# Delta rule: the diagonal blocks of two heads inverted in one pass on 64 partitions

## The chip, the cores and the metric

The kernel runs on one core of a Trainium2 chip. The metric is the time of one execution on the device in microseconds. A core has a matrix engine (PE, with its weight loads shown as PEld), three engines for elementwise work (DVE is VectorE, ACT is ScalarE, POOL is GpSimd) and a queue for transfers that SyncE (SP) issues. Each engine executes its own instruction list in order and waits at semaphores for the others.

## The reference, cut to what matters

One layer of a streaming encoder, for 1024 tokens of width 1024: three mixers (chunked attention A, a Conformer convolution B, a gated delta rule C), merged by three sigmoid gates, then an output projection, a layer norm, an MLP and a second layer norm. The change is in mixer C, which has four heads of width 128:

```
    lmat = jnp.where(strict, jnp.einsum("bnihd,bnjhd->bnhij", kbeta, k) * decay, 0.0)
    tmat = lax.linalg.triangular_solve(eye + lmat, jnp.broadcast_to(eye, lmat.shape),
                                       left_side=True, lower=True, unit_diagonal=True)
    u = jnp.einsum("bnhij,bnjhd->nbhid", tmat, v * beta[..., None])
    w = jnp.einsum("bnhij,bnjhd->nbhid", tmat, kbeta * jnp.exp(gc)[..., None])
...
    def step(state, inp):
        v_new = u_c - jnp.einsum("bhcd,bhde->bhce", w_c, state)
        o_c = (jnp.einsum("bhcd,bhde->bhce", q_c * jnp.exp(g_c)[..., None], state)
               + jnp.einsum("bhij,bhje->bhie", a_c, v_new))
        state = state * jnp.exp(g_last)[..., None, None] + jnp.einsum("bhcd,bhce->bhde", k_dec, v_new)
...
    mix = sum_b sigmoid(gate_b) * (y_b @ W_branch[b])
```

The last line is from the docstring of the layer. `tmat` is the inverse of a lower triangular matrix for each chunk; `step` is a recurrence over the chunks of a head.

## The kernel before, in words

All values are f32. A large product is made of three matmuls on pieces of the operands (high by high, low by high, high by low); the low piece is a subtraction at line 116 (`xl`, `yl` and the like), mostly on DVE or POOL.

Mixer C works with 8 chunks of 128 tokens for each of its heads 0 to 3. A head goes through these steps:

- **dn_a**: `dn_proj` projects, convolves and normalises q, k, v; `dn_s1` makes the triangular matrix `LT`, the masked products `aT`, decays and scales. A row of the decays goes through DRAM and comes back spread over the partitions (L501 and L503 make it, L504 stores it, L452 loads it). The 32x32 blocks on the diagonal of `LT`, four for each of the 8 chunks, are stored to DRAM (`blk_d`, L524).
- **dn_inv**: the 32 blocks are loaded as `X`, one block per partition (L542), and inverted by substitution on DVE: 31 times a product into `tm` (L553) and a subtraction from `X` (L554), the shapes changing each time. POOL clears the upper half (L555), and the result is stored (`inv_d`, L557).
- **dn_b**: `z_load` loads the output gate. `dn_s2` loads the inverted blocks into `T`, transposes them on DVE (L587) and builds the inverse of the whole 128x128 matrix by products `px`, `py`, `px2`, `py2` on PE (all L578), whose results DVE copies out (L592 to L606), then `pu`, `pw`. `dn_scan` is the recurrence: a chunk's step is a matmul with the state (L631), a DVE subtraction (L632), a matmul for the new state (L635), a DVE update of the state `S` (L640); the output matmuls (L633, L642) and their copies on ACT (L643, L644) hang beside it. `dn_out` normalises the head's output (L648, POOL at L190, L655), transposes it on PE (`to`, L659), multiplies by the gate (L660) and stores it to DRAM (`yc_d`, L661).

The merge products follow: `merge(0)`, `merge(1)`, `merge(2)` for mixers A, B and C. Their operands are loaded back from DRAM (`yr`, L719, split into `yh` on ACT at L720 and `yl` at L116); the matmuls write `pbr` (L164 on PE; their weights are named `wbr0x` for A, `wbr1x` for B and `wbr2x` for C, with x for a block of the 1024 output channels, and four k steps are summed, one for each 128 of the 512 channels, so that k step h of C is head h); DVE multiplies by the sigmoid of the gate (L773) and adds (L775, L776). `merge(2)` thus needs the stored output of all four heads.

Two further pieces of work have no tie to the delta rule. Projections of the merge gates (`side_proj`, matmuls that write `fj`, L164 too) are issued at a low priority and put where the scheduler sees room, and so are the convolution steps of mixer B (L676 to L701). The order on each engine is fixed when the program is built: a scheduler takes the operations in program order, by priority and readiness in its own model, so a change of program order moves filling work as well.

Buffers: `dn` is a pool of the phase with one or more buffers for each name; `slot` hands out one of 30 tiles of 128x1024, shared with other stages. PSUM banks: two for `fj`, two for `pbr`, four (`m`) for the delta rule.

Of the kernel before, what the change touches and what calls it, by code (L numbers as in the profile page):

```python
# [9 lines left out]
F32 = mybir.dt.float32  # L10
# [5 lines left out]
P = 128  # L16
T = 1024
# [6 lines left out]
CH = 4  # L24
# [15 lines left out]
def bc_last(ap, n):  # L40
    return bass.AP(tensor=ap.tensor, offset=ap.offset, ap=[list(a) for a in ap.ap] + [[0, n]])


def bc_mid(ap, n):
    a = [list(x) for x in ap.ap]
    return bass.AP(tensor=ap.tensor, offset=ap.offset, ap=[a[0], [0, n]] + a[1:])
# [8 lines left out]
def hybrid_block(ctx, tc, x, xT, pT, w_in, relb, conv_w, conv_b, cln_g, cln_b, dnw, a_log, dt_bias,  # L55
# [3 lines left out]
    V, S, G, PE, SY = nc.vector, nc.scalar, nc.gpsimd, nc.tensor, nc.sync  # L59
# [6 lines left out]
    def phase(name, waits="pool"):  # L66

        if scoped[0] is not None:
            scoped[0].close()
        st = ExitStack()  # L70
        pool = st.enter_context(tc.tile_pool(name=name, bufs=1, reuse_waits=waits))
        scoped[0] = st

        def alloc(shape, dt, tag, bufs, name):
            return pool.tile(shape, dt, tag=tag, bufs=bufs, name=name)

        return alloc
# [8 lines left out]
    def slot(shape, dt=F32, name="g"):  # L86
        return gp.tile(shape, dt, tag="g", bufs=NSLOT, name=name)
# [7 lines left out]
    def bank(tag, shape=(P, 512), name="b"):  # L95
        return ps.tile(list(shape), F32, tag=tag, bufs=NBANK[tag], name=name)
# [324 lines left out]
    def dn_proj(h):  # L421
        res = []
        for i, off in enumerate((O_QC, O_KC, O_VC)):
            w = wrows(w_in, off + P * h, f"wc{h}{i}")
            cw = dnw_s[:, 4 * i + h, :]
            acc = slot([P, T], name=f"c{i}{h}")
            halo = mp.tile([P, 4], F32, tag="halo", bufs=4, name="halo")
            for hf, sl, pp in mm_b(xs, w, name="pc"):
                S.activation(acc[:, sl], pp, AF.Copy, scale=cw[:, 3:4])
                for s_ in (1, 2, 3):  # L430
                    V.scalar_tensor_tensor(acc[:, 512 * hf + s_:512 * hf + 512], pp[:, :512 - s_],  # L431
                                           cw[:, 3 - s_:4 - s_], acc[:, 512 * hf + s_:512 * hf + 512],
                                           ALU.mult, ALU.add)
                    if hf == 1:
                        V.scalar_tensor_tensor(acc[:, 512:512 + s_], halo[:, 3 - s_:3], cw[:, 3 - s_:4 - s_],
                                               acc[:, 512:512 + s_], ALU.mult, ALU.add)
                if hf == 0:
                    V.tensor_copy(halo[:, 0:3], pp[:, 509:512])
            S.activation(acc, acc, AF.Silu)
            res.append(acc)  # L440
        return res

    def ch3(t):
        return t.rearrange("p (c i) -> p c i", i=P)

    def dn_s1(h, qkv):
# [3 lines left out]
        def bcast(src, hf):  # L450
            t = dn([P, 512], F32, "sd", 4, "bc")
            SY.dma_start(t, rows_bcast(src[4 * hf:4 * hf + 1, :], 512))  # L452
            return t

        blk_d = dr.tile([NT, 4, 32, 32], F32, name=f"blk{h}")
        inv_d = dr.tile([NT, 4, 32, 32], F32, name=f"inv{h}")
        brk_d = dr.tile([NT, P], F32, name=f"brk{h}")
        nv = mp.tile([P, 6, NT], F32, tag="nv", bufs=2, name="nv")
        rq, rk, brk, begk, edk = [nv[:, i, :] for i in range(5)]
        LT = dn([P, T], F32, "LT", 1, f"LT{h}")  # L460
        aT = slot([P, T], name=f"aT{h}")
        kdec = slot([P, T], name=f"kdec{h}")
        DTs = []
        for hf in range(2):
# [11 lines left out]
            for i, src in ((1, kT), (0, qT)):  # L476
                tp = bank("pj", name="tk")
                for c4 in range(4):
                    c = hf * 4 + c4
# [3 lines left out]
                for c4 in range(4):  # L483
                    c = hf * 4 + c4
# [3 lines left out]
            for c4 in range(4):  # L488
                c = hf * 4 + c4
# [15 lines left out]
        for hf in range(2):  # L505
# [7 lines left out]
            for c4 in range(4):  # L513
                cs = slice((hf * 4 + c4) * P, (hf * 4 + c4 + 1) * P)
                PE.matmul(kk[:, c4 * P:(c4 + 1) * P], lhsT=kT[:, cs], rhs=kT[:, cs], start=True, stop=True)
            V.tensor_tensor(LT[:, sl], kk, DT, ALU.mult)
            V.tensor_tensor(LT[:, sl], LT[:, sl], bcast(brk_d, hf), ALU.mult)
            kq = bank("pj", name="kq")
# [4 lines left out]
        for d in range(4):  # L523
            SY.dma_start(blk_d[:, d].rearrange("c j i -> j c i"), ch3(LT)[32 * d:32 * d + 32, :, 32 * d:32 * d + 32])  # L524
        for hf in range(2):
# [7 lines left out]
            V.tensor_tensor(ch3(kdec)[:, c8, :], ch3(kdec)[:, c8, :], bc_last(edk[:, c8], P), ALU.mult)  # L533
        return dict(qg=qT, W=kT, vb=vT, LT=LT, aT=aT, kdec=kdec, rq=rq, blk_d=blk_d, inv_d=inv_d)

    def dn_inv(h, o):

        blk_d, inv_d = o["blk_d"], o["inv_d"]
        NB = 32

        X = dn([P, T], F32, "X", 1, "X")
        SY.dma_start(X[:NB, :], blk_d.rearrange("c d j i -> (c d) (j i)"))  # L542
        tm = dn([P, 256], F32, "tm", 1, "tm")
        Xa = X[:NB, :]
        diag = bass.AP(tensor=Xa.tensor, offset=Xa.offset, ap=[list(Xa.ap[0]), [33, 32]])
        V.memset(diag, 1.0)
        X3 = X[:NB, :].rearrange("p (r c) -> p r c", c=32)
        for jj in range(31):
            nr, ncol = 31 - jj, jj + 1
            L = X[:NB, jj * 32 + jj + 1:jj * 32 + 32]  # L550
            R = X3[:, jj, 0:ncol]
            tv = tm[:NB, :nr * ncol].rearrange("p (r c) -> p r c", c=ncol)
            V.tensor_tensor(tv, bc_last(L, ncol), bc_mid(R, nr), ALU.mult)  # L553
            V.tensor_tensor(X3[:, jj + 1:32, 0:ncol], X3[:, jj + 1:32, 0:ncol], tv, ALU.subtract)  # L554
        G.affine_select(out=X3, in_=X3, pattern=[[1, 32], [-1, 32]], compare_op=ALU.is_ge, fill=0.0, base=0,  # L555
                        channel_multiplier=0)
        SY.dma_start(inv_d.rearrange("c d i j -> (c d) (i j)"), X[:NB, :])  # L557

    def dn_s2(h, o):

        LT, inv_d = o["LT"], o["inv_d"]
        T3 = dn([P, T], F32, "T3", 1, "T3")
# [8 lines left out]
        def prod(name, lhsT, rhs, w=P):  # L571

            res = []
            for hf in hfs:
                p = bank("m", name=name)
                for c4 in range(4):
                    l, r = lhsT(hf * 4 + c4), rhs(hf * 4 + c4)
                    PE.matmul(p[0:l.shape[-1], c4 * w:(c4 + 1) * w], lhsT=l, rhs=r, start=True, stop=True)  # L578
                res.append(p.rearrange("p (c d) -> p c d", d=w)[:, 0:4, :])
            return res  # L580

        def chunk(t, c, rows=slice(0, P), c0=0, c1=P):
            return t[rows, c * P + c0:c * P + c1]
# [4 lines left out]

        px = prod("px", lambda c: chunk(LT, c), lambda c: chunk(T3, c))
        for hf in hfs:  # L590
# [24 lines left out]
    def z_load(h, o):  # L615
        z = o["z"] = slot([P, T], name=f"z{h}")
        SY.dma_start(z, z_d[h])
        S.activation(z, z, AF.Silu)
# [28 lines left out]
    def dn_out(h, o, O, ss):  # L647
        V.tensor_scalar(ss, ss, 1.0 / P, RMS_EPS, ALU.mult, ALU.add)  # L648
        r = mp.tile([P, 8], F32, tag="ss", bufs=4, name="r")
        pow_mh(r, ss, 8)  # L650
        for hf in range(2):
            sl = slice(512 * hf, 512 * hf + 512)
            c8 = slice(4 * hf, 4 * hf + 4)
            z = o["z"][:, sl]
            V.tensor_tensor(ch3(O)[:, c8, :], ch3(O)[:, c8, :], bc_last(r[:, c8], P), ALU.mult)  # L655
            tp = bank("m", name="to")
            for c4 in range(4):
                c = hf * 4 + c4
                PE.transpose(tp[:, c4 * P:(c4 + 1) * P], O[:, c * P:(c + 1) * P], ident)  # L659
            V.scalar_tensor_tensor(O[:, sl], tp, ng_s[:, 0:1], z, ALU.mult, ALU.mult)  # L660
            SY.dma_start(yc_d[h][:, sl], O[:, sl])  # L661
# [164 lines left out]
    dn = phase("dn")  # L826

    def dn_a(h):
        return dn_s1(h, dn_proj(h))

    def dn_b(h, o):
        z_load(h, o)
        dn_s2(h, o)
        dn_out(h, o, *dn_scan(h, o))

    st = [None] * CH
    st[0] = dn_a(0)
    dn_inv(0, st[0])
    for h in range(1, CH):
        st[h] = dn_a(h)  # L840
        dn_b(h - 1, st[h - 1])
        dn_inv(h, st[h])
    dn_b(CH - 1, st[CH - 1])
    merge(0, ya_d, True, False)
    merge(1, yb_d, False, False)
    merge(2, yc_d, False, True)
# [331 lines left out]
    dn = phase("down", "tile")  # L1178
# [163 lines left out]
```

## Time and profile before

| quantity | value |
|---|---|
| time, median of 3 runs | 1949.96 us (1948.24 to 1951.97) |
| time of the profiled execution | 1944.56 us |
| span of the profiled execution | 1942.8 us |
| mean granted TensorE clock, share of full | 0.982 |
| PE busy | 1850.1 us, 95% of the span |
| DVE busy | 1258.3 us, 65% |
| ACT busy | 831.1 us, 43% |
| POOL busy | 445.0 us, 23% |

The span lies within the execution's own time, which has 1.8 us around it. Shares are means over all stages; the delta rule runs from about 518 us to 1030 us after the span's start, with the first merges inside its last part.

### The profile page before, as it was taken

What the parts mean: (1) busy time and instruction counts of PE and PEld (TensorE: products, weight loads), DVE (VectorE), ACT (ScalarE), POOL (GpSimd) and SP (SyncE); (2) the same over time, 40 slices, a digit from 0 to 9 for tenths busy, and PEclk for the clock granted to TensorE, in tenths of its full rate; (3) what the DMA queues carried; (4) which work ended last, traced back from release to release, by engine and by line L of the source; (5) the groups of instructions that cost most, each with busy time, mean ns of one, the idle gap of its engine ahead of it and who ended that gap; (6) DMA issues with size and microseconds to landing.
All of it is one profiled execution on the core that took longest, in us unless ns stands there. A gap on an engine that the chain in (4) does not pass through costs nothing. (4 is left out here: it accounts for less than half of the span.)

```text
span 1942.8 us, 25812 instructions
## 1 busy us (share of the span) xinstructions
PE 1850.1 (95%) x9265; PEld 1543.4 (79%) x9265; DVE 1258.3 (65%) x2203; ACT 831.1 (43%) x1516; POOL 445.0 (23%) x373
## 2 busy tenths in 40 slices
PE   8999999989999989989999999989999989999996
PEld 7988887778777878777877997768888877878775
DVE  3248969989957857664377367763333327865978
ACT  4454544446324343442344237435555553333333
POOL 2123423334322122212121142223232310000001
PEclk9999999999999989999999999999999999999998
DMA  6212222232242332333354435763333367542442
GB/s 200 82 53 68 74 64 72 65 87 87 87 117 60 98 90 84 92 111 107 125 190 163 155 123 188 246 211 130 104 114 108 109 233 251 214 162 97 175 152 87
DMA packets 207793, 244.68 MB, mean 126 GB/s; under 512 B 23792, under 2 KB 126256, under 8 KB 207664
## 3 DMA queue, kind: packets, MB, share of 16 engines
q1 hardware_dynamic: 207664, 243.03, 38.6%
q8 instruction: 73, 1.20, 0.2%
q14 instruction: 56, 0.46, 0.1%
HBM read 183.17 MB, written 59.80 MB: 125 GB/s over the span
## 5 line engine op out<-in xcount | busy, mean ns | idle before, releaser
L676 DVE SCALAR_TENSOR_TENSOR ca<-ci,cw_s,ca 128x512 f32<-128x512 f32 x240 | 214.2, 892 | 3.8
L986 PE MATMUL pda<-bh,ah 128*128 128x512 f32 x256 | 97.6, 396 | 9.1 <-DVE x L1246 5.1
L987 PE MATMUL pda<-bl,ah 128*128 128x512 f32 x256 | 100.6, 393 | 0.0
L988 PE MATMUL pda<-bh,al 128*128 128x512 f32 x256 | 100.4, 393 | 0.0
L190 POOL TENSOR_TENSOR mv<-mv,nhalf 128x1 f32<-128x1 f32 x16 | 17.4, 1094 | 360.9 <-DVE mv L683 360.9
L307 POOL TENSOR_SCALAR st<-st,mx 128x640 f32<-128x640 f32 (+2 forms) x64 | 58.7, 919 | 179.8 <-DVE mx L306 174.2
L304 ACT ACTIVATE st<-st,mx 128x640 f32<-128x640 f32 (+2 forms) x64 | 44.5, 696 | 117.0 <-DVE mx L300 116.8
L986 PE MATMUL pdb<-bh,ah 128*128 128x512 f32 x192 | 74.6, 401 | 7.0 <-DVE x L1246 7.0
L1204 ACT ACTIVATE ah<-draw 128x1024 fp32r<-128x1024 f32 x32 | 33.9, 1061 | 102.9 <-PE pda L987 51.2
L1157 DVE TENSOR_TENSOR r<-puc,r 128x512 f32<-128x512 f32 x16 | 11.1, 692 | 103.1 <-PE puc L988 103.1
L987 PE MATMUL pdb<-bl,ah 128*128 128x512 f32 x192 | 76.4, 398 | 0.0
L988 PE MATMUL pdb<-bh,al 128*128 128x512 f32 x192 | 75.9, 398 | 0.0
L986 PEld LDWEIGHTS pda<-bh,ah 128*128 128x128 f32 x256 | 48.6, 190 | 20.9 <-ACT bh L1204 7.3
L988 PEld LDWEIGHTS pda<-bh,al 128*128 128x128 f32 x256 | 48.7, 190 | 10.4
L987 PEld LDWEIGHTS pda<-bl,ah 128*128 128x128 f32 x256 | 48.7, 190 | 10.2 <-DVE bl L116 0.2
L553 DVE TENSOR_TENSOR tm<-X 32x31 f32<-32x31 f32 (+15 forms) x124 | 53.4, 431 | 3.0
L116 DVE TENSOR_TENSOR al<-draw,ah 128x1024 fp32r<-128x1024 f32 x32 | 39.1, 1221 | 22.7 <-ACT ah L1204 22.7
L431 DVE SCALAR_TENSOR_TENSOR c<-pc,dnw_s,c 128x511 f32<-128x511 f32 (+2 forms) x72 | 52.5, 731 | 0.1
L554 DVE TENSOR_TENSOR X<-X,tm 32x31 f32<-32x31 f32 (+15 forms) x124 | 50.1, 404 | 3.0
L771 ACT ACTIVATE sgl<-sgl 128x512 f32<-128x512 f32 x48 | 30.2, 631 | 50.0 <-DMA sgl<-sg_d 41.5
L334 ACT ACTIVATE ph<-tp 128x512 fp32r<-128x512 f32 (+2 forms) x72 | 37.0, 525 | 32.0 <-PE tp L330 27.5
L116 POOL TENSOR_TENSOR wu2l<-wu,wu2h 128x512 fp32r<-128x512 f32 x16 | 20.8, 1303 | 128.1 <-ACT wu2h L866 128.1
(1605 smaller groups left out, 6199.7 us busy)
## 6 DMA issues: line engine op xcount, KB each, us to landing
draw<-h_d SPq DMA_DIRECT2D x48, 512.0 KB, 5.0
wu<-in_w_up_dram SPq DMA_DIRECT2D x32, 512.0 KB, 3.9
h_d<-r SPq DMA_DIRECT2D x64, 256.0 KB, 2.1
draw<-in_w_down_dram SPq DMA_DIRECT2D x32, 512.0 KB, 4.6
sg_d<-fs SPq DMA_DIRECT2D x48, 256.0 KB, 2.1
sgl<-sg_d SPq DMA_DIRECT2D x48, 256.0 KB, 2.8
wg<-in_w_pg_dram SPq DMA_DIRECT2D x36, 256.0 KB, 4.3
cb<-in_w_down_dram SPq DMA_DIRECT2D x16, 512.0 KB, 8.1
```

What stands on the lines that cost most here:

```text
L116: eng.tensor_tensor(lo, src, hi.bitcast(F32), ALU.subtract)
L304: S.activation(st[:, :nk], st[:, :nk], AF.Exp, scale=-1.0, bias=mx[:, nm:nm + 1], accum_out=mx[:, 2:3])
L307: G.tensor_scalar(st[:, :nk], st[:, :nk], mx[:, 3:4], 1.0, ALU.mult, ALU.mult)
L334: S.activation(ph[:, :n], tp[:, :n], AF.Copy)
L431: V.scalar_tensor_tensor(acc[:, 512 * hf + s_:512 * hf + 512], pp[:, :512 - s_], cw[:, 3 - s_:4 - s_], acc[:, 512 * hf + s_:512 * hf + 512 ...
L553: V.tensor_tensor(tv, bc_last(L, ncol), bc_mid(R, nr), ALU.mult)
L554: V.tensor_tensor(X3[:, jj + 1:32, 0:ncol], X3[:, jj + 1:32, 0:ncol], tv, ALU.subtract)
L676: V.scalar_tensor_tensor(acc, t[:, H - s_:H - s_ + 512], cw_s[:, i, H - s_:KB - s_], acc, ALU.mult, ALU.add)
L986: PE.matmul(out_, lhsT=ah, rhs=bh, start=first, stop=False, skip_group_check=True)
L987: PE.matmul(out_, lhsT=ah, rhs=bl, start=False, stop=False, skip_group_check=True)
L988: PE.matmul(out_, lhsT=al, rhs=bh, start=False, stop=last, skip_group_check=True)
L1204: S.activation(hi, src, AF.Copy)
```

## The change

`dn_inv` takes a list of two heads. Two loads fill 64 partitions of `X`, the 62 DVE operations, the memset and the mask run once for both heads, and two stores write the result. `LT` lives from `dn_a` of its head to `dn_b`, and two heads now wait between the two, so it moves from a one-buffer tile to a slot. The program order of the heads becomes a0, a1, inversion of 0 and 1, b0, a2, b1, a3, inversion of 2 and 3, b2, b3, where it was a0, inv0, a1, b0, inv1, a2, b1, inv2, a3, b2, inv3, b3.

```diff
@@ -457,7 +457,7 @@
         brk_d = dr.tile([NT, P], F32, name=f"brk{h}")
         nv = mp.tile([P, 6, NT], F32, tag="nv", bufs=2, name="nv")
         rq, rk, brk, begk, edk = [nv[:, i, :] for i in range(5)]
-        LT = dn([P, T], F32, "LT", 1, f"LT{h}")
+        LT = slot([P, T], name=f"LT{h}")
         aT = slot([P, T], name=f"aT{h}")
         kdec = slot([P, T], name=f"kdec{h}")
         DTs = []
@@ -533,13 +533,13 @@
             V.tensor_tensor(ch3(kdec)[:, c8, :], ch3(kdec)[:, c8, :], bc_last(edk[:, c8], P), ALU.mult)
         return dict(qg=qT, W=kT, vb=vT, LT=LT, aT=aT, kdec=kdec, rq=rq, blk_d=blk_d, inv_d=inv_d)
 
-    def dn_inv(h, o):
-
-        blk_d, inv_d = o["blk_d"], o["inv_d"]
-        NB = 32
+    def dn_inv(os_):
+
+        NB = 32 * len(os_)
 
         X = dn([P, T], F32, "X", 1, "X")
-        SY.dma_start(X[:NB, :], blk_d.rearrange("c d j i -> (c d) (j i)"))
+        for n, o in enumerate(os_):
+            SY.dma_start(X[32 * n:32 * n + 32, :], o["blk_d"].rearrange("c d j i -> (c d) (j i)"))
         tm = dn([P, 256], F32, "tm", 1, "tm")
         Xa = X[:NB, :]
         diag = bass.AP(tensor=Xa.tensor, offset=Xa.offset, ap=[list(Xa.ap[0]), [33, 32]])
@@ -554,7 +554,8 @@
             V.tensor_tensor(X3[:, jj + 1:32, 0:ncol], X3[:, jj + 1:32, 0:ncol], tv, ALU.subtract)
         G.affine_select(out=X3, in_=X3, pattern=[[1, 32], [-1, 32]], compare_op=ALU.is_ge, fill=0.0, base=0,
                         channel_multiplier=0)
-        SY.dma_start(inv_d.rearrange("c d i j -> (c d) (i j)"), X[:NB, :])
+        for n, o in enumerate(os_):
+            SY.dma_start(o["inv_d"].rearrange("c d i j -> (c d) (i j)"), X[32 * n:32 * n + 32, :])
 
     def dn_s2(h, o):
 
@@ -834,13 +835,15 @@
         dn_out(h, o, *dn_scan(h, o))
 
     st = [None] * CH
-    st[0] = dn_a(0)
-    dn_inv(0, st[0])
-    for h in range(1, CH):
-        st[h] = dn_a(h)
-        dn_b(h - 1, st[h - 1])
-        dn_inv(h, st[h])
-    dn_b(CH - 1, st[CH - 1])
+    st[0], st[1] = dn_a(0), dn_a(1)
+    dn_inv(st[0:2])
+    dn_b(0, st[0])
+    st[2] = dn_a(2)
+    dn_b(1, st[1])
+    st[3] = dn_a(3)
+    dn_inv(st[2:4])
+    dn_b(2, st[2])
+    dn_b(3, st[3])
     merge(0, ya_d, True, False)
     merge(1, yb_d, False, False)
     merge(2, yc_d, False, True)
```

The lines behind `dn_inv` stand one further down in the changed kernel (L631 becomes L632, L659 becomes L660, L773 becomes L774).

The list of PE during the recurrence of head 3, before (`c_7845` and `c_7768` are the k and q tiles of head 3; the matmuls before and after these rows are `pbr` too):

```order
L164 MATMUL pbr<-yh,wbr13h 128x512
L164 MATMUL pbr<-yl,wbr13h 128x512
L164 MATMUL pbr<-yh,wbr13l 128x512
L631 MATMUL scan<-S,c_7845 128x128
L633 MATMUL scano<-S,c_7768 128x128
L164 MATMUL pbr<-yh,wbr14h 128x512
L164 MATMUL pbr<-yl,wbr14h 128x512
L164 MATMUL pbr<-yh,wbr14l 128x512
```

And after, for the same recurrence, its last steps (`c_7788`, `c_7711`, `c_7634` are the v, k and q tiles of head 3), up to its output:

```order
L636 MATMUL scan<-c_7788,kdec_7859 128x128
L643 MATMUL scano<-c_7788,aT_7858 128x128
L632 MATMUL scan<-S,c_7711 128x128
L634 MATMUL scano<-S,c_7634 128x128
L636 MATMUL scan<-c_7788,kdec_7859 128x128
L643 MATMUL scano<-c_7788,aT_7858 128x128
L632 MATMUL scan<-S,c_7711 128x128
L634 MATMUL scano<-S,c_7634 128x128
L643 MATMUL scano<-c_7788,aT_7858 128x128
L660 MATMUL to<-ident,c_7788 128x128 x8
L164 MATMUL pbr<-yh,wbr20h 128x512
L164 MATMUL pbr<-yh,wbr21h 128x512
```

Between the steps there stood matmuls of the merges of A and B, and now stands nothing; the matmuls behind the output transposes `to` are those of `merge(2)`.

PE at the end of head 2, before (`c_7291` is its v tile; `T_8390`, `LT_7991` belong to head 3):

```order
L659 MATMUL to<-ident,c_7291 128x128 x8
L578 MATMUL px<-T_8390,LT_7991 128x128 x8
L164 MATMUL pbr<-yl,wbr00h 128x512
L164 MATMUL pbr<-yh,wbr00l 128x512
L164 MATMUL pbr<-yh,wbr00h 128x512
L164 MATMUL pbr<-yl,wbr00h 128x512
L164 MATMUL pbr<-yh,wbr00l 128x512
```

And after (`c_7225` is head 2's v tile, `T_8258`, `TT_8264`, `LT_7857` belong to head 3):

```order
L634 MATMUL scano<-S,c_7071 128x128
L643 MATMUL scano<-c_7225,aT_7295 128x128
L660 MATMUL to<-ident,c_7225 128x128 x8
L579 MATMUL px<-T_8258,LT_7857 128x128 x8
L579 MATMUL py<-TT_8264,T_8258 128x128 x8
L164 MATMUL pbr<-yh,wbr20h 128x512
L164 MATMUL pbr<-yh,wbr21h 128x512
L164 MATMUL pbr<-yl,wbr20h 128x512
L164 MATMUL pbr<-yh,wbr20l 128x512
```

Behind the first products of head 3 stood `merge(0)` with its weights `wbr00`, and before `py` 17 such matmuls; now `py` follows `px` directly, and then come matmuls of `merge(2)` (`wbr20`, `wbr21`), which take head 2's output as it comes back from DRAM.

DVE in the middle of an inversion, before (that of head 3; `c_7291` is head 2's v tile in its recurrence, `bst`, `bmv` belong to mixer B):

```order
L553 TENSOR_TENSOR tm<-X 32x135
L696 BN_STATS bst<-tb 128x6
L632 TENSOR_TENSOR c_7291<-c_7291,scan 128x128
L554 TENSOR_TENSOR X<-X,tm 32x27x5
L682 BN_AGGR bmv<-bst 128x2
L553 TENSOR_TENSOR tm<-X 32x156
L683 TENSOR_SCALAR bmv<-bmv 128x1
L640 SCALAR_TENSOR_TENSOR S<-S,egl,scan 128x128
```

And after, in the second of the two inversions (`mix` is the merged output, `pbr` a product of `merge(0)`):

```order
L553 TENSOR_TENSOR tm<-X 64x192
L774 TENSOR_TENSOR mix_8489<-pbr,sgl 128x512
L554 TENSOR_TENSOR X<-X,tm 64x24x8
L774 TENSOR_TENSOR mix_8530<-pbr,sgl 128x512
L774 TENSOR_TENSOR mix_8489<-pbr,sgl 128x512
L553 TENSOR_TENSOR tm<-X 64x207
L554 TENSOR_TENSOR X<-X,tm 64x23x9
L553 TENSOR_TENSOR tm<-X 64x220
```

The inversion shared DVE with the recurrence of the head before; it now shares it with the merge of A, and no recurrence runs beside it.

## Rows read from the trace of the kernel before

**Rows 1.** The page, part 1: busy time, share of the span, instructions.

```profile
PE 1850.1 (95%) x9265; PEld 1543.4 (79%) x9265; DVE 1258.3 (65%) x2203; ACT 831.1 (43%) x1516; POOL 445.0 (23%) x373
```

**Rows 2.** Two stretches: length, busy PE, PEld, DVE, ACT, POOL; clock, DMA share, GB/s.

```profile
560.00:882.00 322.00, 293.77 (x1550) 244.25 (x1550) 234.41 (x578) 124.54 (x314) 74.68 (x62) 0.95 0.31 90
882.00:1000.00 118.00, 116.75 (x593) 97.00 (x592) 49.70 (x101) 44.63 (x94) 21.35 (x16) 1.00 0.44 143
```

**Rows 3.** Waits of PE, 560 to 882: total us, times, longest us.

```profile
PE scan L631 <- DVE S L640: 7.2, 5, 3.9
PE scan L635 <- DVE c L632: 5.5, 5, 3.6
PE tv L490 <- ACT tk L485: 3.1, 1, 3.1
PE pc L164 <- DVE halo L438: 3.0, 1, 3.0
```

**Rows 4.** The page, part 5: the inversion, busy us, mean ns, idle before.

```profile
L553 DVE TENSOR_TENSOR tm<-X 32x31 f32<-32x31 f32 (+15 forms) x124 | 53.4, 431 | 3.0
...
L554 DVE TENSOR_TENSOR X<-X,tm 32x31 f32<-32x31 f32 (+15 forms) x124 | 50.1, 404 | 3.0
```

**Rows 5.** Timeline, DVE: start, duration, operation; one on 32 partitions.

```profile
925.60 0.28 DVE L597 TENSOR_SCALAR TT<-py 32x128 f32<-32x128 f32 x1 [4.23 <-PE py L578]
```

**Rows 6.** Timeline: a step of the recurrence that nothing covers.

```profile
803.66 0.35 DVE L640 SCALAR_TENSOR_TENSOR S<-S,egl,scan 128x128 f32<-128x128 f32 x1
...
804.59 0.29 DVE L632 TENSOR_TENSOR c<-c,scan 128x128 f32<-128x128 f32 x1 [0.30 <-PE scan L631]
...
804.93 0.49 PE L635 MATMUL scan<-c,kdec 128*128 128x128 f32 x2 [0.16 <-DVE c L632]
...
805.68 0.34 DVE L640 SCALAR_TENSOR_TENSOR S<-S,egl,scan 128x128 f32<-128x128 f32 x1
```

**Rows 7.** Timeline, PE: two matmuls back to back.

```profile
1028.15 0.39 PE L164 MATMUL pbr<-yh,wbr20h 128*128 128x512 f32 x1
...
1028.38 0.39 PE L164 MATMUL pbr<-yl,wbr20h 128*128 128x512 f32 x1
```

**Rows 8.** Timeline: the output of head 2.

```profile
909.53 0.39 PE L642 MATMUL scano<-c,aT 128*128 128x128 f32 x2
...
912.63 1.29 DVE L655 TENSOR_TENSOR c<-c,r 128x512 f32<-128x512 f32 x2 [1.76 <-POOL r L190]
...
917.91 1.03 PE L659 MATMUL to<-ident,c 128*128 128x128 f32 x8
```

**Rows 9.** Head 3's output through DRAM to PE; then landing times of `yc_d`.

```profile
1020.07 0.93 SPq L661 DMA_DIRECT2D yc_d<-c  x2
...
1028.84 0.50 PE L164 MATMUL pbr<-yh,wbr20h 128*128 128x512 f32 x1
...
DMA to landing us min/median/max: 2.0/4.2/6.1
```

**Rows 10.** Timeline, heads 2 and 3: decay row, start and end of an inversion, transposes.

```profile
736.43 0.28 DVE L503 COPY vr<-vp 8x128 f32<-8x128 f32 x1 [2.30 <-PE vp L501]
...
753.39 0.09 DVE L546 MEMSET X<- 32x32 f32 x1
...
833.38 0.28 DVE L503 COPY vr<-vp 8x128 f32<-8x128 f32 x1
...
853.19 0.09 DVE L546 MEMSET X<- 32x32 f32 x1
...
888.07 1.26 POOL L555 TENSOR_SCALAR_AFFINE_SELECT X<-X 32x1024 f32<-32x1024 f32 x1 [9.62 <-DVE X L554]
...
894.82 1.30 DVE L587 STREAM_TRANSPOSE TT<-T 128x512 f32<-128x512 f32 x2
```

**Rows 11.** DVE by line: the merge's product.

```profile
L773 DVE TENSOR_TENSOR mix<-pbr,sgl 128x512 f32<-128x512 f32 x16 | 10.9, 690 | 18.8 <-PE pbr L164 15.9 <-DMA sgl<-sg_d 2.3 <-ACT sgl L771 0.6
```

**Rows 12.** Timeline, PE: one matmul at the lower clock.

```profile
703.09 0.63 PE L164 MATMUL fj<-xl,fg17h 128*128 128x512 f32 x1
```

## The prediction

> **What bounds the kernel now.** The page comes first: PE is busy for 95% of the span [rows 1], so what the change does to the time is what it does to PE's idle time and to its clock. The windows come next, over the delta rule: from 560 to 882 us PE is busy for 293.77 of 322 us, so 28.2 us are idle, and its granted clock is 0.95 of full; from 882 to 1000 us it is busy for 116.75 of 118 at a clock of 1.00 [rows 2]. The second stretch holds the last part of head 2's recurrence, and head 3's products and most of its recurrence: they cost nothing there, because the merges of A and B fill every gap. The waits of PE say what the 28.2 us are: 12.7 for the steps of the recurrences (7.2 and 5.5), 3.1 for the decays of a head, 3.0 for the convolution, and small ones [rows 3]. DVE is late in them, and the inversion is part of what keeps it: 53.4 and 50.1 us in all, with 248 operations [rows 4]. So there is something to gain, but a bounded thing: 28.2 us of idle PE and, with a clock of 0.95 over 322 us, some 16 us of PE's speed.
>
> **What is removed.** Four inversions of 62 operations become two. An operation on 32 partitions with 128 elements took 0.28 us [rows 5], one on 128 partitions with 128 elements 0.29 us [rows 6]: the partitions cost nothing, so an inversion of 64 partitions takes (53.4+50.1)/4 = 25.9 us, as one of 32 did. DVE loses 51.8 us of work. The two memsets and masks that go, and the transfers, whose number stays (a load and a store for each head), are off PE's path; `LT` in a slot costs nothing where no slot has to be waited for, and the order shows no operation that is put off for one. I price these at 0; a late slot would cost what a late head costs, below.
>
> **What is moved, and its price.** PE's list keeps its work: the same matmuls, 1850 us. What moves is the filling. Before, nine to twenty matmuls of the merges of A and B stand in each half step of head 3's recurrence. Now the merge of A stands under the second inversion and the merge of B under head 2, and nothing is left for head 3: its 30 matmuls stand back to back, behind them `to`, and behind that `merge(2)`, which needs `to`'s result. I sum this tail as path less PE's own work.
>
> A step that nothing covers took from one state update to the next 2.02 us, with other DVE work in it; its four parts alone are 0.49, 0.29, 0.49 and 0.35 (L631's matmul taken like L635's), so 1.62 [rows 6]. I take 1.85, since a semaphore stands between the parts. PE's own work in a step is two pairs of 0.39 [rows 8].
> - Head 2's last 2.5 steps, for which the filling has run out: 4.6 less 2.0 is 2.7.
> - Head 2's output: from the last product to the scaling 3.1 us (909.53 to 912.63), half of the scaling 0.65, the transposes 1.03 [rows 8] and hops of 0.2: 5.0, less 1.0, is 4.0. Before, this had cover.
> - Head 3's products. On PE, `px` and `py` go ahead, and then 12 matmuls of `merge(2)` that take head 2's output through DRAM; `px2` stands behind the first of them, and on DVE two of head 3's small transposes stand behind the two splits of that output. From the store to the first matmul head 3's trip took 8.8 us (1020.07 to 1028.84); two transfers at the shortest landing, 2.0 each, and about 1 for the split between make 5 [rows 9]. I take 7. The rest, with 0.7 for the second split [rows 11], is the exchange of PE and DVE from `py` to `pw`: I estimate 7.4, from halves of groups of 1.03 [rows 8] and copies near 0.3 [rows 5] with hops. Together 15.1, less PE's six groups of 1.03 and 12 matmuls at 0.23 [rows 7], 9.0, is 6.1.
> - Head 3's recurrence: 0.9 for the first chunk and six more steps, 12.0, less 15 pairs of 0.39, 5.9, is 6.1.
> - Its output and trip: 5.0 and 7.0, less 1.0, is 11.0. PE can't run ahead of it, for `merge(2)` has two `pbr` banks, both of which stand waiting for the last k step, head 3.
>
> The tail is 30 us (24 with steps of 1.62 and trips of 5; 35 with 2.02 and 8.8).
>
> Then the two inversions, each of which now keeps two heads waiting. From the decay row to the inversion it took 19.8 us for head 3 and 17.0 for head 2, mean 18.4; from its mask to the first transposes 6.8 (888.07 to 894.82) [rows 10].
> - Second one: 18.4 + 25.9 + 6.8, and about 19 of the merge's and split's operations on DVE between them at 0.69 [rows 11], 13.1: 64 us from head 3's decay row to head 2's `px`. In this piece PE has 192 matmuls of the merge of A at 0.23 [rows 7], 44.2, and 4.2 of small ones: 48. Idle: 16.
> - First one: 18.4 + 25.9 + 6.8 and 8 of convolution work on DVE, 59, against 192 matmuls at 0.23 and 30 small ones, 48. Idle: 11.
> - What stays as it was: 3.1 for a head's decays and 3.0 for the convolution [rows 3], about 6.5 for the recurrences of heads 0 and 1 (half of 12.7, since DVE has no inversion beside them), 1.5 for head 2's products.
>
> That is 41 us against 28.2 before, so 13 more. Clock: a matmul at the lower level took 0.63 us [rows 12] where the same form takes 0.39 [rows 7]; I count 4 us of PE work after the tail at that rate, 2.5 more. Sum: 30 + 13 + 2.5 = 45. The profiled execution took 1944.56 us, so 1990; the median of the runs is 5.4 us above that execution, which I leave in the range.
>
> **The Trainium skill against the trace.** The Trainium skill, "VectorE: DVE Perf Modes", section "Rules for kernel authors", says that for a chain of VectorE operations the number of operations is what to bring down. The trace agrees as far as [rows 5, 6] go. By it the change should gain; that is the faster rival below. The Trainium skill, "TensorE: Matmul & The Clock Gate", section "What's actually happening", says that the matrix engine is throttled by default and that activity lifts this, which speaks against a tail full of gaps. The trace agrees: 0.95 in the stretch with 28.2 us idle and 1.00 in the full one [rows 2]. By it the tail runs at 1.2 GHz; that is the dear rival.
>
> **The rivals.**
> - *The tail alone.* The new waits at the inversions are repaid by the 51.8 us that DVE loses: heads 0 and 1 run with a freer DVE, and PE's idle there stays at 28 or falls to 15. For it: DVE is busy for 234 of 322 us in that stretch, and its lateness is 12.7 us of waits [rows 2, 3]. Against it: the 18.4 before an inversion and the 6.8 after are transfers and queues, which do not shrink. Time: 1944.6 + 24 to 35, less up to 13: 1960 to 1976.
> - *The dear tail.* The clock falls in the tail. Then a matmul takes 1.6 times as long (0.63 for 0.39) [rows 7, 12], 0.8 for 0.49 [rows 6]: the 17 on the path of the two recurrences add 0.3 each, 5; the eight groups of 1.03 on the path add 0.6 each, 5; the matmuls of `merge(2)` add 3. That is 13 more: 2003, to 2016 with the tail's upper bound and 8 more at the inversions. For it: the gaps there come one behind the other. Against it: in the recurrences before, with waits of up to 3.9 us [rows 3], the clock over the whole stretch stayed at 0.95.
> - *Faster.* The shorter DVE list ends the waits of the recurrences and of the decays and lifts the clock: at most 28.2 + 16 us are there. The place is 560 to 882; it decides from the point at which it saves more than the tail's 24 to 35, and PE must then be idle there for less than about 3 us. Against it: the waits for the two inversions are in that very stretch. If all of it were saved and the tail were at its lower end, 1944.6 + 24 - 44 = 1925; in the middle about 1935.
> - *Nothing.* The tail is covered by work that the order does not show as such, or the savings equal it: 1945 to 1955.
>
> **How the numbers follow.** Chances: the forecast, 1976 to 2003, 0.58; the tail alone 0.15; the dear tail 0.18; faster 0.05; nothing 0.04. The likeliest is 1990. The range leaves out the two last, 0.09, and the outer quarter of the two beside the forecast, 0.08: 1964 to 2014. A measurement of this kernel tells about 0.2%, 4 us, from no change: faster 0.05, within it 0.04, slower 0.91.
>
> **What would show it.** In the profile after: DVE's busy time near 1258 - 52 = 1206 us; 62 + 62 operations of the inversion with a mean near 420 ns; PE's busy share near 93%; waits of PE for head 3's state and for `yh` near the end of the delta rule, with a sum near 25 to 35 us where the stretch of [rows 2] had 1.2; two waits of PE's `px` for the transposes or for the inverted blocks, 16 and 11 us long. It is wrong if PE's order as built does not lead to waits, that is if the stretch of head 3 has steps well under 1.6 us, or if the wait for the second inversion is near 0.

## The result, and the profile after

The changed kernel takes 1977.45 us (median of 4 runs, 1975.45 to 1980.25) against 1949.85 before: 1.0142 times, 95% interval 1.0124 to 1.016, so 27.6 us slower. The forecast was 1990, in a range of 1964 to 2014. The profiled execution has a span of 1973.7 us, 30.9 more than before. Two disturbed runs, one of 3083 us of a later experiment and one of 6460 us of the kernel before, count in no time and no ratio below.

The first view is the page of the changed kernel: busy time, share of the span, instructions; then the two groups of the inversion.

```profile
PE 1859.3 (94%) x9265; PEld 1552.0 (79%) x9265; DVE 1204.1 (61%) x2077; ACT 833.5 (42%) x1515; POOL 445.4 (23%) x371
...
L554 DVE TENSOR_TENSOR X<-X,tm 64x31 f32<-64x31 f32 (+15 forms) x62 | 25.8, 416 | 1.5
L553 DVE TENSOR_TENSOR tm<-X 64x31 f32<-64x31 f32 (+15 forms) x62 | 24.5, 395 | 1.7
```

The change does on DVE what it says: half the operations at the same 0.4 us each, on twice the partitions; DVE is busy for 54.2 us less than in [rows 1]. And it is slower all the same. PE has the same 9265 records; it is idle for 1973.7 - 1859.3 = 114.4 us, against 1942.8 - 1850.1 = 92.7 before, 21.7 more; and its busy time is 9.2 longer, from stretches at a lower clock and from matmuls that stand alone. The two make the 30.9.

The windows of the changed kernel say where. Columns as in [rows 2]; the cuts are head 1's decay row (620.4), head 0's products (686), head 0's and head 1's outputs (768, 872), head 3's decay row (882), head 2's products (948), and a time near the end of its recurrence (1010).

```profile
518.00:620.40 102.40, 99.28 (x468) 80.84 (x467) 47.68 (x102) 38.35 (x89) 29.47 (x25) 0.98 0.32 92
620.40:686.00 65.60, 53.57 (x244) 43.50 (x244) 47.30 (x115) 17.87 (x31) 14.42 (x13) 0.92 0.40 107
686.00:768.00 82.00, 79.35 (x439) 66.43 (x439) 27.91 (x69) 29.60 (x81) 18.05 (x16) 1.00 0.28 82
768.00:872.00 104.00, 104.00 (x564) 87.21 (x563) 42.54 (x109) 40.44 (x104) 23.51 (x20) 1.00 0.29 89
872.00:882.00 10.00, 2.63 (x18) 1.99 (x16) 3.02 (x10) 7.09 (x22) 2.91 (x1) 0.80 0.33 108
882.00:948.00 66.00, 53.99 (x233) 44.38 (x233) 48.54 (x111) 24.00 (x37) 12.23 (x9) 0.89 0.55 167
948.00:1010.00 62.00, 61.38 (x323) 51.19 (x323) 40.37 (x68) 24.01 (x48) 11.39 (x9) 0.99 0.48 150
1010.00:1068.00 58.00, 41.25 (x232) 33.32 (x231) 23.79 (x55) 14.70 (x46) 3.61 (x3) 0.83 0.14 46
```

Three stretches stand out. Under each of the two inversions PE is idle for 12.0 us (65.60 - 53.57, 66.00 - 53.99), and for 7.4 just before the second. In the last row, the end of head 2 and head 3's own stretch, it is idle for 16.8 us of 58, at a clock of 0.83. Between them PE is nearly full (2.65 us idle from 686 to 872, 0.62 from 948 to 1010). DVE is never near full: 48.54 of 66 us at most.

The waits of PE from 518 to 1060 us, columns as in [rows 3]; the smaller of the two waits for `yh` is the start of a longer one, cut off at 1060:

```profile
PE pbr L164 <- ACT yh L721: 10.2, 2, 9.5
PE tq L702 <- DVE bcv L699: 8.6, 2, 8.4
PE to L660 <- DVE c L656: 6.9, 2, 3.5
PE tv L490 <- ACT tk L485: 4.7, 1, 4.7
PE kk L515 <- DVE c L492: 3.0, 1, 3.0
PE vp L501 <- DVE nv L497: 2.7, 1, 2.7
PE scan L632 <- DVE S L641: 2.5, 10, 0.6
PE px L579 <- DMA T<-inv: 2.4, 1, 2.4
```

The recurrence waits of [rows 3], 12.7 us, are down to some 5, in many short pieces: with no inversion beside them the steps are answered at once. In their place stand waits for other things that are late: the operand of the merge of A, the norm of mixer B, each head's output. The timeline of the tail shows the pieces of it in order:

```profile
1024.47 3.62 PE L579 MATMUL px<-T,LT 128*128 128x128 f32 x16
...
1027.88 2.12 PE L579 MATMUL py<-TT,T 128*128 128x128 f32 x16
...
1038.71 1.95 PE L579 MATMUL pw<-TT,c 128*128 128x128 f32 x16
...
1041.64 0.49 PE L632 MATMUL scan<-S,c 128*128 128x128 f32 x2 [0.54 <-DVE S L639]
...
1043.51 0.49 PE L632 MATMUL scan<-S,c 128*128 128x128 f32 x2 [0.22 <-DVE S L641]
...
1057.38 1.97 PE L660 MATMUL to<-ident,c 128*128 128x128 f32 x8 [3.45 <-DVE c L656]
1065.08 0.80 PE L164 MATMUL pbr<-yh,wbr20h 128*128 128x512 f32 x1 [5.74 <-ACT yh L721]
```

A bare step takes about 1.8 us (43.51 - 41.64 is 1.87, the next five 1.81 on average); head 3's output waits 3.45 us for its scaling, is transposed in 1.97 where [rows 8] had 1.03, and comes back from DRAM 5.74 us later. The first matmul of the last k step takes 0.80 us where [rows 7] has 0.39: PE is at the lower of its levels, 1.2 GHz, after these gaps: its granted clock is 0.50 from 1065.08 to 1069 us.

### The profile page after: what moved, and what is told of

Read it like the earlier page. It is cut to its first block, busy times and chain, and to the rows that moved or that the text cites. A ratio compares the mean times of both kernels' runs of the same rounds, so it can differ in the third digit from the quotient of the medians.

```text
span 1973.7 us, 25685 instructions
## 1 busy us (share of the span) xinstructions
PE 1859.3 (94%) x9265; PEld 1552.0 (79%) x9265; DVE 1204.1 (61%) x2077; ACT 833.5 (42%) x1515; POOL 445.4 (23%) x371
## 5 line engine op out<-in xcount | busy, mean ns | idle before, releaser
L990 PEld LDWEIGHTS pda<-bl,ah 128*128 128x128 f32 x256 | 48.7, 190 | 10.2
L989 PEld LDWEIGHTS pdb<-bh,ah 128*128 128x128 f32 x192 | 37.2, 194 | 16.0 <-issue 8.2
L116 DVE TENSOR_TENSOR pl<-tp,ph 128x512 fp32r<-128x512 f32 (+2 forms) x72 | 42.4, 593 | 8.8 <-ACT ph L334 8.1
```

What stands on the lines that cost most here:

```text
L116: eng.tensor_tensor(lo, src, hi.bitcast(F32), ALU.subtract)
L989: PE.matmul(out_, lhsT=ah, rhs=bh, start=first, stop=False, skip_group_check=True)
L990: PE.matmul(out_, lhsT=ah, rhs=bl, start=False, stop=False, skip_group_check=True)
```

## The experiments

The theory that they set out from: the joint inversion makes head 2 wait until head 3 has its decays and its blocks. The delta rule's way through the heads, which was half hidden, becomes one chain from head 3's decays to its output; PE's filling is spent under the wait, and the end of the chain stands bare. The rivals: the new order of the heads or the slots cost; or the length of the shared inversion does. All times are medians; ratios are to the kernel before, with 95% intervals.

**Order and slots without the grouping.**

```diff
-    dn_inv(st[0:2])
+    dn_inv(st[0:1])
+    dn_inv(st[1:2])
...
-    dn_inv(st[2:4])
+    dn_inv(st[2:3])
+    dn_inv(st[3:4])
```

> The program order of the heads and LT in a slot stay as in the changed kernel, but each head has an inversion of its own on 32 partitions. My theory (the joint inversion makes head 2 wait for head 3, and the filling work is used up under that wait, so that head 3's products, recurrence and output stand bare): the list of PE has matmuls of the merges in head 3's recurrence again, and the time is that of the kernel before, 1945 to 1958 us. Rival (the new order of the heads, or two LT in slots, costs): it stays near the changed kernel, 1970 to 1980 us.

Measured: 1949.54 us, ratio 1.0002 (0.9988 to 1.0017). The program order of the heads and two more slots cost nothing: the scheduler goes by what is ready, and puts each head's inversion under the head before it, as in the kernel before (the four inversions begin at 568.9, 655.4, 759.7 and 858.8 us; before at 569.5, 652.1, 753.4 and 853.2). The whole price is that one instruction works for two heads.

**The inversion made shorter, and longer.** In the second inversion alone, 1 step of 31, or the 31 steps twice:

```diff
-    def dn_inv(os_):
+    def dn_inv(os_, steps=31):
...
-        for jj in range(31):
+        for jj in range(steps):
...
-    dn_inv(st[2:4])
+    dn_inv(st[2:4], 1)
```

> The second inversion does 1 of its 31 steps (the output of heads 2 and 3 is not the reference's); the rest as in the changed kernel. It takes 25 us of DVE work off the way from head 3's decays to head 2's first product. My theory (the price lies in the bare tail of head 3, which this leaves as it is, and in the wait for the operand of the merge of A at the start of that stretch): little is won, 1966 to 1977 us. Rival (the two heads' wait for a long inversion is the price): the time falls by the 25 us, to about 1952.

```diff
-    def dn_inv(os_):
+    def dn_inv(os_, rep=1):
...
-        for jj in range(31):
+        for jj in list(range(31)) * rep:
...
-    dn_inv(st[2:4])
+    dn_inv(st[2:4], 2)
```

> The second inversion's 31 steps are done twice in a row (the output of heads 2 and 3 is not the reference's), 26 us more of DVE work between head 3's decays and head 2's first product. My theory (from head 3's decays to the end nothing else but this chain sets the time): nearly all of it is seen, 1996 to 2006 us, since the filling is used up anyhow. Rival (PE's filling covers the inversion, and its length hardly counts): below 1988 us.

Measured: 1964.96 us (1.0078, 1.0049 to 1.0107) and 2000.41 (1.0254, 1.0233 to 1.0276). The longer one is as expected, 23 of its 26 us are seen. In its timeline PE has spent the merge of A and a part of that of B, and then stands:

```profile
980.35 2.90 PE L579 MATMUL px<-T,LT 128*128 128x128 f32 x12 [17.92 <-DMA T<-inv]
```

The shorter one gives back 12.5 us of its 25, one more than the most I expected and half of what the rival said: I had not counted that with `px` earlier (911.7 in place of 946.4 us) 48 of the 192 matmuls of the merge of A are spent ahead of it in place of all of them, and more are left for head 2 (its trace has no wait before head 2's output). The wait of 9.4 us at the start and the bare tail of head 3 stay. So the inversion's length counts nearly fully upward and by half downward: at its present length it is on the chain. What stops the gain at half was not taken apart.

**Heads 2 and 3 through the recurrence in turn.**

```diff
-    dn_b(2, st[2])
-    dn_b(3, st[3])
+    dn_bb([(2, st[2]), (3, st[3])])
...
+    def dn_bb(hos):
+        for h, o in hos:
+            z_load(h, o)
+            dn_s2(h, o)
+        dn_scans(hos)
+        for h, o in hos:
+            dn_out(h, o, o["vb"], o["ss"])
```

`dn_scans` is `dn_scan` with the loop over heads inside that over chunks, and two `S` tiles for each head.

> Heads 2 and 3 also go through the rest together: products of both, then the two recurrences step by step in turn, then both outputs; all else as in the changed kernel. My theory (the bare tail is the price): each recurrence fills the other's gaps, the second trip through DRAM goes, and of the tail's 26 us of idle time about half is left: 1958 to 1968 us. Rival (the waits at the two inversions are the price, and the tail is not): 1974 to 1980 us.

Measured: 1961.8 us (1.0073, 1.0051 to 1.0094), as the theory said. The windows of this run, from a bare piece of the two recurrences to the matmuls behind the outputs:

```profile
1029.13:1038.00 8.87, 8.87 (x72) 8.30 (x71) 5.22 (x17) 5.71 (x25) 0.00 (x0) 1.00 0.00 0
1038.00:1055.00 17.00, 8.89 (x32) 7.27 (x33) 8.29 (x14) 3.64 (x10) 3.24 (x2) 0.60 0.37 124
```

With no filling at all two recurrences keep PE busy (8.87 of 8.87 us at full clock): each is the other's cover. What is left is the joint output and its trip, 8 us idle at a clock of 0.60. Of the 13.8 us between the profiled executions of the changed kernel and of this run, 10.1 are PE's busy time (1859.3 to 1849.2 for the same 9265 records: fewer of them stand alone or run at the lower clock). Only 3.7 are idle time, since other waits grew (that of `px` is 4.6 us here, 2.4 in the changed kernel).

**Both pairs so.** Heads 0 and 1 go through it in turn as well.

```diff
-    dn_b(0, st[0])
-    st[2] = dn_a(2)
-    dn_b(1, st[1])
-    st[3] = dn_a(3)
+    dn_bb([(0, st[0]), (1, st[1])])
+    st[2] = dn_a(2)
+    st[3] = dn_a(3)
```

> As the run with the recurrences of heads 2 and 3 in turn, and heads 0 and 1 in the same manner, so that heads 2 and 3 begin only when both of these are done. My theory: the tail is that of the other run; the first pair's recurrences are covered by the gate projections either way, and heads 2 and 3's projections have work of their own: 1955 to 1970 us. Rival (the delta rule needs one head's recurrence under the next head's inversion, and pairing all the way takes the last cover away): slower than the run with one pair, 1975 to 1990 us.

Measured: 1965.5 us (1.0086, 1.0058 to 1.0114), within what the theory gave, and nothing won over the one pair: there was no bare recurrence among heads 0 and 1 to cover (PE is idle for 2.65 us from 686 to 872 in the changed kernel).

**The wait for the merge's first operand.** In the changed kernel two activations for the output gates of heads 2 and 3 stand on ACT's list ahead of that operand's split, and wait for their load; the first of them is

```profile
892.07 1.06 ACT L619 ACTIVATE z<-z 128x1024 f32<-128x1024 f32 x1 [11.81 <-DMA z<-z_d]
```

The edit loads the gate into the tile of `LT`, which comes free only after the products:

```diff
-        z = o["z"] = slot([P, T], name=f"z{h}")
+        z = o["z"] = o["LT"]
...
-        z_load(h, o)
         dn_s2(h, o)
+        z_load(h, o)
```

> The output gate of a head is loaded into the tile of LT after its products, so its activation no longer stands on ACT's list ahead of the split of the merge's first operand; else the changed kernel. In the trace of the changed kernel PE waits 9.5 us for that split at the start of the second inversion's stretch. My theory: the way from head 3's decays to the end of the delta rule is a chain that these 9.5 us do not lie on; PE will only wait for the inversion later, or run out of filling sooner: 1972 to 1980 us. Rival (this wait is a price by itself, to be had back): 1965 to 1970 us.

Measured: 1970.98 us (1.0114, 1.0091 to 1.0136), between the two. The wait of 9.5 us is 2.8; another of 3.2 comes where the merge of B begins, and the tail is as bare as before. Two thirds of the wait were a price of their own; the theory's "nothing" was wrong.

**Something else left to do under head 3.** The merge of C takes head 2's output in place of head 3's:

```diff
-                SY.dma_start(raw, dram[i][:, sl])
+                SY.dma_start(raw, dram[i if dram is not yc_d else min(i, 2)][:, sl])
```

> The merge of mixer C takes head 2's output in place of head 3's in its last k step (the output is not the reference's), so that nothing behind waits for head 3; its work stays. My theory (the tail is bare because all that is left needs head 3): the matmuls of that merge go under head 3's recurrence, 156 of them at 0.23 us are 36 us of cover for some 26 of idle time, and the time falls to 1948 to 1956 us. Rival (the price is paid at the inversions): 1970 us or more.

Measured: 1979.41 us (1.0145, 1.0124 to 1.0166): nothing won, and my expectation missed by 23 us. The trace says why. The filling did go under head 3's recurrence, but much more of it to a step than a step needs: three of the steps began at

```profile
1058.21 0.38 PE L632 MATMUL scan<-S,c 128*128 128x128 f32 x2
...
1070.26 0.38 PE L632 MATMUL scan<-S,c 128*128 128x128 f32 x2
...
1080.44 0.38 PE L632 MATMUL scan<-S,c 128*128 128x128 f32 x2
...
1091.31 0.79 PE L636 MATMUL scan<-c,kdec 128*128 128x128 f32 x2 [4.50 <-DVE c L633]
...
1103.19 1.12 PE L660 MATMUL to<-ident,c 128*128 128x128 f32 x4 [3.46 <-DVE c L656]
```

10 to 12 us apart, where a bare step takes 1.8. So the filling was gone with the last steps and the output still to come; they stand bare again, now ahead of the output projection on PE's list, with a wait of 4.5 us for a DVE that splits the merged output. The dependence on head 3 was not the reason that I took it for: the filling is spent before the chain is through, whatever it is.

**Some filling held back.** The weights of the second half of the merge of B are scaled by a one that comes from head 2's output:

```diff
-        S.activation(hi, raw, AF.Copy)
+        S.activation(hi, raw, AF.Copy, scale=1.0 if hold is None else hold)
...
+        if h == 2:
+            hold[0] = dn([P, 1], F32, "hold", 1, "hold")
+            V.tensor_scalar(hold[0], r[:, 0:1], 0.0, 1.0, ALU.mult, ALU.add)
...
+                        hold=hold[0] if b == 1 and d >= 4 else None)]
```

> The changed kernel, with the second half of the merge of B held back: its weights are scaled by a one that is made from head 2's finished output, so that 96 of its 192 matmuls are left for head 3. My theory (the filling is given out some 20 matmuls to a half step, until none is left, so that holding some back only moves the bare steps from head 3 to head 2): 25 recurrence matmuls of head 2 and 23 of head 3 stand bare in the list, and the time stays, 1972 to 1983 us. Rival (head 3 alone lacks cover, and giving it some is what it needs): 1958 to 1967 us.

Measured: 1981.26 us (1.016, 1.0125 to 1.0195), three runs. The bare steps move (head 2's last six and head 3's last five now wait for the state, where it was two and seven), and the time doesn't fall, as the theory that the runs had by then said. PE's waits from 940 to 1070 us in this run:

```profile
PE to L665 <- DVE c L661: 7.7, 2, 4.2
PE pbr L164 <- ACT yh L726: 6.4, 1, 6.4
PE scan L634 <- DVE S L643: 2.8, 11, 0.7
PE px L581 <- DMA T<-inv: 2.8, 1, 2.8
```

**The trip through DRAM.** On the run with heads 2 and 3 in turn, the merge of C splits the heads' tiles themselves:

```diff
-            SY.dma_start(yc_d[h][:, sl], O[:, sl])
+        ycs[h] = O
...
-            yr = slot([P, T], name="yr")
+            yr = slot([P, T], name="yr") if dram is not None else ycs[i]
...
-    merge(2, yc_d, False, True)
+    merge(2, None, False, True)
```

> The run with the recurrences of heads 2 and 3 in turn, and the merge of C splits its operand from the heads' output tiles instead of from a copy that went through DRAM. In that run's trace PE waits 5.2 us for the trip and 2.9 for the scaling behind it, and then works at a low clock. My theory: the trip goes, and the scheduler puts matmuls of the merge of B beside the outputs: 1949 to 1957 us. Rival (what is won there is lost to another wait at once): 1958 to 1965 us.

Measured: 1953.65 us (1.0005, 0.9991 to 1.002), 8.2 less by the medians: the tail's last two waits, 2.9 and 5.2 us, are gone. With the gate in `LT`'s tile as well:

> As the run without the trip through DRAM, and the output gate goes into LT's tile after the products, which took away the 9.5 us wait at the start of the second inversion's stretch in an earlier run and 6.5 us of the time. My theory: the gains add up, 1943 to 1952 us, at least the kernel before's time. Rival (with the waits for the operand gone PE waits for the inversion instead): 1952 to 1958 us.

Measured: 1950.77 us (0.9998, 0.9982 to 1.0015). The pairing is back at the kernel before, not past it. The 6.5 us of the gate's edit became some 3, which the two intervals do not tell from nothing: the operand waits are still 4.5 and 3.3 us there.

**What these two edits do to the kernel before**, without any pairing. The gate in `LT`'s tile, with `LT` in a slot:

> The kernel before with LT in a slot and the output gate loaded into it, inversions one by one: a slot less for each head. In its list of PE the merge of C has 30 matmuls ahead of head 3's output and no stretch is bare. My theory: PE is the bound from head 2's recurrence on, and what it waits for before that hardly changes: 1943 to 1952 us, that is no change or a little faster. Rival (a later load of the gate adds waits for it): 1953 us or more.

Measured: 1952.45 us (1.0024, 1.0008 to 1.004), at the edge of what I gave: no gain. The operand from the tiles:

> The kernel before, its merge of C taking the heads' output from their tiles as in the other two runs. In the kernel before the trip through DRAM is under the merge of B, with 0.2 us of wait. My theory: no change, 1946 to 1953 us; what the trip costs in the changed kernel comes from the missing cover. Rival (the trip costs by itself, for instance by its transfers): 1940 to 1945 us.

Measured: 1933.91 us (0.9906, 0.9885 to 0.9928), faster than both kernels and faster than either side had said. Its window and waits from 560 to 882 us, to be laid beside [rows 2, 3]:

```profile
560.00:882.00 322.00, 299.63 (x1594) 249.58 (x1593) 231.24 (x588) 123.27 (x312) 77.92 (x64) 0.97 0.31 87
```

```profile
PE scan L631 <- DVE S L640: 5.8, 5, 3.9
PE tq L701 <- DVE bcv L698: 5.0, 4, 2.1
...
PE scan L635 <- DVE c L632: 0.8, 3, 0.5
```

The trip itself was covered before (from 882 us on PE waited 1.3 us for `yh` and `yl`), so its going can't be the whole gain. PE is idle for 22.4 us in this stretch in place of 28.2, the wait of L635 falls from 5.5 to 0.8, and the clock is 0.97 for 0.95. The profiled executions are 10.6 us apart, 6.3 of idle time and 4.3 of PE's busy time; the medians are 16 apart. The edit also frees four slots and moves the list of every engine; which of these ended that wait was not taken apart. And it changes what the runs above are worth: with the operand taken from the tiles on both sides, the joint inversion with heads 2 and 3 in turn is at 1953.65 us against 1933.91 with four inversions. Without the pairing it was 1977.45 against 1949.85; the pairing didn't close the gap.

## Why the prediction was right, and where its sizes were off

The mechanism held in the main: the joint inversion is the cause (without it the same order costs nothing), the tail is bare, PE stands idle under each inversion, and DVE's relief doesn't pay for it. The sum, 45 us, was 14 too high. The time alone doesn't tell the forecast from its nearest rival: the median, 1977.45, is at the lower edge of the forecast's 1976 to 2003, and the profiled execution, 1975.45, at the upper end of the 1960 to 1976 of the tail alone (whose terms as written reach from 1956 to 1980). The windows tell them apart: ahead of the tail PE's idle time rose by 7.6 us, where that rival had no rise and the forecast 13.

- *The signs.* DVE's time, the mean of its operations and PE's share came as forecast. Two did not: the waits of `px`, 16 and 11 us in the forecast, were 2.4 and none, and the tail's idle time was 16.8 where 25 to 35 were forecast. By that wait alone the second inversion would nearly have counted as covered; that its length counts is shown by the run with 31 steps more.
- *The partitions cost nothing.* Right: 395 and 416 ns for an operation on 64 partitions against 431 and 404 [rows 4]; DVE at 1204.1 us, forecast 1206.
- *The chain at the second inversion.* Right to a microsecond: 64 us were forecast from head 3's decay row to head 2's `px`; it began at 883.14 and `px` at 946.37, 63.2. The idle time is 12.0 and not 16, and it lies elsewhere: 9.5 of it in front of the merge's matmuls that I had counted as cover from the start, since ACT held their operand back behind the gates. Only 2.4 are left at `px`.
- *The first inversion.* 59 us forecast, idle 11; it took 61.4 (624.19 to 685.60), and the idle time was 12.0. That the two idle times agree is luck, for `px` did not wait at all: 8.4 us are a transpose of mixer B that waits for an operation which DVE's list has late in the inversion, with matmuls of the gate projections queued behind it, and 3.0 are products of head 1 (`kk`) that wait for DVE.
- *What stays as it was.* Too much: 6.5 us for the recurrences of heads 0 and 1, measured 2.65 and 0 (the windows from 686 to 872). Here DVE's relief did show. On the other side 7.4 us of waits came ahead of head 3's decay row, where I had 3.1. All of it up to 1010 us: 37.8 us of idle time (the first seven windows), forecast 41; before there were 28.2 and 2.0 around them. So 7.6 more, where I had 13. The sum of this part came near because terms that were too high and terms that were missing made up for each other.
- *The tail.* Its way was forecast at 4.6 + 5.0 + 15.1 + 12.0 + 12.0 = 48.7 us; from the first bare step (1014.41) to the first matmul of the last k step (1065.08) it took 50.7. The step of 1.85 was 1.81, the trip of 7 was 5.7, the products of 15.1 were 16 at a partly lower clock. What failed is the step "less PE's six groups of 1.03": a group's eight matmuls are sixteen records on PE, 1.95 to 2.1 us in the rows above, since only the transposes go through once (of the six, `py2` on 64 partitions is shorter, 1.26). PE's own work in the tail is some 5 us more than the 18.9 that I took off, and its idle time so much less: 16.8 us in the window, to which some 9 are to be added for matmuls that are longer at the lower clock or stand alone (41.25 us busy, where the same records take about 31, an estimate from the mean of each kind in the covered stretches; 1.4 of the difference lies behind the tail). With this term right the tail is 25 to 26 us in place of 30.
- *The clock.* Forecast as 2.5 us after the tail; the nine matmuls at 0.63 and 0.80 from 1065.08 to 1069 take 3.9 us where they would take 2.1 at 0.23, so 1.8. But the tail itself also ran at 0.83, with `px` at 3.62 us after head 2's output. The rival of the dear tail had the effect right and its size too high.
- The rest of the kernel, outside 518 to 1068 us, has 2.6 us less of idle time, which is no part of the change that I can name.

The Trainium skill, "VectorE: DVE Perf Modes", section "Rules for kernel authors", tells to lower the number of VectorE operations in a chain. The trace agrees for DVE, 54 us less; the time went the other way, since DVE, busy for 61% of the span, was not the bound, and what the change took away was the work that had covered PE's waits.

What is open: why the kernel before gains 16 us from the operand taken out of the tiles, and what stops the gain of the shorter inversion at half.

## What to carry to other kernels

An instruction that serves two items of a pipeline makes the first wait for the second. Before merging work, look at what runs under each of the two now, and at what will run under the one. That an engine ends many of the waits, as DVE did here, is not enough for its relief to pay. The list scheduler here gave each gap of a serial chain far more filling than it needed, so that filling was spent from the front and the chain's end stood bare, with half of it held back as well. Two chains run against each other covered each other with no filling at all; but that alone bought back only about half of what the grouping had cost.

## What the runs showed of the hardware

An inversion's operation on DVE takes 0.17 to 0.42 us by its size; but 21 of 248 before took 1.03 to 1.51, and 6 of 124 after took 1.15 to 1.40. Every one of these ran beside a subtraction on POOL and ended 0.04 to 0.28 us after it. Three more before and seven after took 0.59 to 0.99, beside a POOL operation that had begun earlier. The timeline of the changed kernel, DVE and POOL:

```profile
656.72 1.54 POOL L116 TENSOR_TENSOR wc310l<-wc310r,wc310h 128x512 fp32r<-128x512 f32 x1 [10.63 <-ACT wc310h L133]
657.14 1.39 DVE L553 TENSOR_TENSOR tm<-X 64x256 f32<-64x256 f32 x1
...
658.57 0.42 DVE L554 TENSOR_TENSOR X<-X,tm 64x256 f32<-64x256 f32 x1
```

The DVE operation ends at 658.53, POOL's at 658.26, and the next one of the same size takes 0.42 again: it was held for as long as POOL's worked. This agrees with the Trainium skill, "SBUF — State Buffer", section "SBUF: two separate sides", by which a VectorE operation with two inputs in SBUF and a GpSimd operation that reads SBUF exclude each other for a whole instruction. With half the operations there are about half the delays, 13 in place of 24: one operation in ten both times.
